# Normalised fp16 parts of x for the query, u and gate products of a hybrid attention and gMLP block, in a written order

## The chip, the cores and the metric

The kernel runs on one core of a Trainium2 chip. The metric is the time of one execution on the device in microseconds, and the figure for a kernel is the median of its runs. The core has five engines that run side by side, each with its own stream of instructions: PE (TensorE, the matrix products; its weight loads are listed apart as PEld), DVE (VectorE), ACT (ScalarE), POOL (GpSimd) and SP (SyncE, which issues most transfers). An instruction that needs another engine's result waits for it, and everything behind it on its engine waits too.

## The reference, cut to what matters

The block has 1024 tokens and a width of 1024. One projection of the RMS-normalised input feeds attention, a gated MLP over positions, and two merge gates.

```python
h = rmsnorm(x, norm_gain)                       # x * rsqrt(mean(x^2)) * gain
q, k, v, gate_a, u_in, v_in, gate_b, g_merge = split(h @ w_in)   # 512,128,128,512,512,512,512,2048
q = axial_rope(rmsnorm(q, q_gain)); k = axial_rope(rmsnorm(k, k_gain))   # 8 q heads, 2 kv heads, 64 each
attn = block_attention(q, k, v) * silu(gate_a)  # softmax over all 1024 keys
y_a = attn @ w_proj_attn
vv = layernorm(gelu(v_in)) in 8 chunks of 128 tokens, 8 groups of 64 channels
v_mix = w_spatial (128x128 per group) applied over the positions of a chunk, + b_spatial
gm = gelu(u_in) * v_mix * silu(gate_b)
y_b = gm @ w_proj_gmlp
g = sigmoid(g_merge + b_merge)                  # two gates, 1024 columns each
y = g[0] * y_a + g[1] * y_b
out = rmsnorm(x + y @ w_out, final_gain)
```

## The kernel before, in words

**Products in parts.** Every fp32 product is made of three matmuls: each operand is split into a rounded part (hi) and the remainder (lo), and `mm3` adds hi·hi, hi·lo and lo·hi in PSUM. In most of the kernel the parts are fp32r; in the softmax weights and in the merge gates they are fp16. A split is a cast on ACT (L112) and a subtraction (L118) on DVE or, for the weights of u, gate_a and gate_b, on POOL.

**x.** `load_x` brings the transposed x in eight tiles of 128 channels, multiplies by the gain and splits into `xh`, `xl` (fp32r, 16 tiles of 512 KB, resident until the gates). They are not yet normalised. The key-value, v, q, u, gate_a and gate_b products all read them, and the factor 1/rms of each token (`rstd`) is applied to each result: in the activation for v, in the head norms for q and k, and by a DVE multiply with the row `rB` after each u or gate product (L511, L494). The mean squares come from a second load of x, rows as tokens, squared on ACT (`add_square`, L171). `rB` is made at the end of the q products (L475).

**Stages.** The key-value products (`mm3` with 256 columns) run while x arrives. Then come four v groups and the position mixing `spatial` (sp), then four q groups with the head norm, the rotary table and transposes to `qT` (`q_post`). Attention is 64 units (one head, 128 queries): a score product (L550, L551) into one of three PSUM tiles of tag S, a row maximum on DVE (L553), an exponential on ACT (L557), a reciprocal, a hi part on ACT (L563) and a lo part on DVE (L564), and a transposing transfer T<-p on the SP queue. Two units make one `mix` with the values (L576). Between the units lie 24 **fills**: u, gate_a and gate_b, four column tiles each and two halves of 512 tokens, 24 matmuls a half (L488 to L490). Their weights come by `stream_w`: hi on ACT, lo on POOL. After attention come eight products with the gMLP projection (`proj_b`, yb), then for each of eight column tiles a pair of merge gates (`pair`, g) by a scheme with seven block products in place of eight (`seven`), the attention projection ya by the same scheme, and the output product with the final norm.

**Gates.** Before the gates x is loaded a third time and, chunk by chunk (`x_chunk`), normalised and made into the seven forms the scheme needs, each split to fp16 (`make_forms`). The weights of a pair are brought to unit size first: `pair_weights` loads two 512 KB tiles, squares them on ACT, sums over the partitions with four one-column matmuls (usg, L671), and POOL takes the power (L673 to L677, tile scg); `split16` then makes hi on ACT (L682) and lo on DVE (L683).

**Order.** The order of the work is that of the code as a scheduler then places it on each engine: `plan` spreads the fills over the units, and `MORDER` lists the gate and projection steps (in it, w0 stands right before g0).

## Time and profile before

| quantity | value |
|---|---|
| time, median of three runs | 736.19 us (736.14 to 736.78) |
| profiled execution, its own time | 736.99 us |
| span of the profiled execution | 735.2 us |
| PE busy | 714.0 us, 97% of the span |
| DVE, ACT, POOL busy | 565.9, 431.2, 110.4 us |
| granted PE clock, mean | 0.992 |

The profiled execution took 1.8 us more than its span and 0.8 us more than the median of the runs. Busy PE time contains the slack between pipelined matmuls, so that 97% does not say that PE runs at its best pace in every stage. The share of DVE is an average too: it differs from stage to stage.

The stages, as the first instruction of each on PE marks them, in microseconds from the start of the span: key-value and v products 5.4 to 82; q products, position mixing and k transposes 82 to 135.7; the first 32 score products 135.7 to 265.6; the others 265.6 to 386.7; gMLP projection 386.7 to 450.1; gates and attention projection 450.1 to 618.8; output 618.8 to 735.2.

### The profile page before, as it was taken

The page shows a single profiled execution, that of the slowest core. Times are in us where ns is not written, and L with a number is a line of the kernel's source. Part 1 is how long each engine was busy: PE and PEld are TensorE (multiplying, and loading weights), DVE is VectorE, ACT ScalarE, POOL GpSimd, SP SyncE. Part 2 cuts the span into 40 slices and gives each one's busy share as a digit, 9 for nine tenths or more (in the row PEclk, how much of TensorE's full clock was granted, in tenths as well). Part 3 has the DMA queues.
Part 4 walks back from the last instruction along what each step waited for, and adds up shares of the span by engine and source line. Part 5 has one row for each costly group of instructions (what it writes and reads, how often), then busy time and mean ns, then how long its engine had stood idle before and what let it go on. Part 6 is the DMA issues. An engine that isn't in the chain of part 4 may idle for free.

```text
span 735.2 us, 11836 instructions
## 1 busy us (share of the span) xinstructions
PE 714.0 (97%) x4633; PEld 531.4 (72%) x4633; DVE 565.9 (77%) x822; ACT 431.2 (59%) x770; POOL 110.4 (15%) x101
## 2 busy tenths in 40 slices
...
GB/s 307 317 129 1 115 16 43 1 122 94 150 157 182 176 180 167 183 170 175 154 245 287 132 30 14 45 129 15 46 98 58 0 1 184 157 146 1 114 30 86
DMA packets 152904, 85.59 MB, mean 116 GB/s; under 512 B 135440, under 2 KB 136080, under 8 KB 152848
## 3 DMA queue, kind: packets, MB, share of 16 engines
...
q10 hardware_dynamic: 288, 0.28, 0.1%
...
## 4 chain that ended last, share of the span: by engine, by line
PE 83%; DVE 5%; ACT 5%; DMA 5%; issue 1%; POOL 1%; SPq 0%; POOLq 0%; ACTq 0%; DVEq 0%
PE o L576 5%; PE out L175 4%; DMA T<-p 4%; PE out L176 4%; PE out L174 4%; PE s L550 3%; PE s L551 3%; PE g L174 3%; PE g L175 3%; PE g L176 3%; PE gb L488 2%; PE q L174 2%; PE q L175 2%; PE v L175 2%; PE v L174 2%; PE q L176 2%
## 5 line engine op out<-in xcount | busy, mean ns | idle before, releaser
L564 DVE SCALAR_TENSOR_TENSOR p<-P,ri,p 128x1024 f16<-128x1024 f32 x64 | 83.4, 1304 | 26.4 <-ACT p L563 26.3
L557 ACT ACTIVATE P<-s,nm 128x1024 f32<-128x1024 f32 x64 | 71.2, 1113 | 24.2 <-DVE nm L553 20.8
L563 ACT ACTIVATE p<-P,ri 128x1024 f16<-128x1024 f32 x64 | 73.1, 1145 | 15.7 <-DMA T<-p 8.8
L553 DVE TENSOR_REDUCE nm<-s 128x1 f32<-128x1024 f32 x64 | 77.6, 1214 | 3.0 <-PE s L551 2.9
L576 PEld LDWEIGHTS <-vS 128*64 128x64 f16 x1536 | 45.3, 111 | 19.0 <-issue 17.8
L576 PE MATMUL o<-T,vS 128*64 128x128 f16 x1536 | 52.0, 222 | 4.2 <-DMA T<-p 3.8
L118 POOL TENSOR_TENSOR wl<-wraw,wh 128x512 fp32r<-128x512 f32 x24 | 39.9, 1665 | 97.7 <-ACT wh L112 55.6
L550 PE MATMUL s<-kT,qT 128*128 128x512 f32 x128 | 52.9, 413 | 0.0
L551 PE MATMUL s<-kT,qT 128*128 128x512 f32 x128 | 50.9, 397 | 0.0
L911 ACT ACTIVATE sq<-xr 128x1024 f32<-128x1024 f32 x7 | 7.4, 1062 | 65.4 <-DVE xr L969 65.4
L969 DVE TENSOR_TENSOR xr<-out,xr 128x1024 f32<-128x1024 f32 x7 | 8.6, 1224 | 47.6 <-PE out L176 47.5
L674 POOL TENSOR_SCALAR scg<-scg 128x1 f32<-128x1 f32 x8 | 6.5, 807 | 206.7 <-ACT scg L673 206.6
L550 PEld LDWEIGHTS s<-kT,qT 128*128 128x128 f32 x128 | 24.3, 189 | 6.3 <-issue 0.2
L551 PEld LDWEIGHTS s<-kT,qT 128*128 128x128 f32 x128 | 24.3, 190 | 5.4 <-issue 0.2
L112 ACT CAST wh<-wraw 128x512 fp32r<-128x512 f32 x35 | 21.4, 616 | 10.4 <-PE ga L489 3.4
L682 ACT ACTIVATE wg<-graw,scg 128x512 f16<-128x512 f32 x16 | 11.4, 721 | 26.6 <-PE g L176 13.2
L488 PE MATMUL ga<-xh,wh 128*128 128x512 f32 x64 | 26.0, 406 | 0.8 <-DVE ga30w L494 0.5
L488 PE MATMUL u<-xh,wh 128*128 128x512 f32 x64 | 25.8, 402 | 0.0
L488 PE MATMUL gb<-xh,wh 128*128 128x512 f32 x64 | 25.5, 399 | 0.0
L175 PE MATMUL yb<-gml,wh 128*128 128x512 f32 x64 | 25.5, 398 | 0.0
L490 PE MATMUL u<-xh,wl 128*128 128x512 f32 x64 | 25.4, 397 | 0.0
L490 PE MATMUL gb<-xh,wl 128*128 128x512 f32 x64 | 25.4, 396 | 0.0
...
## 6 DMA issues: line engine op xcount, KB each, us to landing
...
graw<-in_wall_dram SPq DMA_DIRECT2D x16, 512.0 KB, 5.8
xraw<-in_xT_dram SPq DMA_DIRECT2D x13, 512.0 KB, 6.4
xn<-in_x_dram SPq DMA_DIRECT2D x8, 512.0 KB, 6.3
wor<-in_wall_dram SPq DMA_DIRECT2D x8, 512.0 KB, 5.1
xr<-in_x_dram SPq DMA_DIRECT2D x8, 512.0 KB, 3.8
out_dram<-xr SPq DMA_DIRECT2D x7, 512.0 KB, 2.6
...
```

What stands on the lines that cost most here:

```text
L174: pe.matmul(o, ah, bh, start=start, stop=False)
L175: pe.matmul(o, ah, bl, start=False, stop=False)
L176: pe.matmul(o, al, bh, start=False, stop=stop)
L488: pe.matmul(o, wh[:, C(dt % 4)], xh[dt][:, H(h)], start=(dt == 0), stop=False)
L490: pe.matmul(o, wl[:, C(dt % 4)], xh[dt][:, H(h)], start=False, stop=(dt == 7))
L550: pe.matmul(sp[:, H(hf)], qs, kT[:, 2 * v, H(hf)], start=True, stop=False)
L551: pe.matmul(sp[:, H(hf)], qs, kT[:, 2 * v + 1, H(hf)], start=False, stop=True)
L553: dve.tensor_reduce(out=nm, in_=sp, axis=AX.X, op=ALU.max, negate=True)
L557: act.activation(Pt, sp, AF.Exp, bias=nm, accum_out=rsum)
L563: act.activation(hi, Pt, AF.Copy, scale=ri)
L564: dve.scalar_tensor_tensor(out=lo, in0=Pt, scalar=ri, in1=hi, op0=ALU.mult, op1=ALU.subtract)
L576: pe.matmul(ot[64 * h:64 * h + 64, 0:128], vS[:, kt, v, 64 * vl:64 * vl + 64], T[:, h, 8 * p + kt, :], start=(n == 0), stop=(n == len(part ...
```

## The change

The fp32r parts `xh`, `xl` stay for the key-value and v products only. x is squared in its transposed tiles as it arrives (ACT, two of them on POOL), summed on DVE, and eight one-column matmuls (`sst`) give the mean squares, so that `rstd` and `rB` stand during the v products; the loads of x by rows are gone. The transposed x is loaded again in four pairs of 512 KB tiles, multiplied by `rB` (three tiles on DVE, five in halves on POOL) and split into resident fp16 parts `x16` (eight casts of 1024 on ACT, eight subtractions on DVE). q, u, gate_a and gate_b become fp16 products of `x16` with weights that are first scaled to unit size, as the gates already did. The scales need the weights once more: `scales` loads those of q and of the first four fill tiles in eight 512 KB transfers issued by the ACT queue, into the tiles of the squares, and those of the other eight in sixteen 256 KB transfers on the SP queue, and squares them on ACT. One group of four matmuls (usq) gives q's scale and the first four of the fills, three groups of two (usu, usa, usb) the others. `split16` makes their parts, hi on ACT and lo on DVE, in place of POOL's subtraction. The DVE multiply by `rB` after a fill is gone for the gates (`silu2` takes the scale in the Tanh) and is a multiply by a scalar for u; the scale of gate_b enters where gm is split, that of gate_a in `avs`. The gates take three of their seven forms from `x16`, so that `x_chunk` splits four and not seven. gm is split within the attention stage, and the weights of the first gate pair (`pair_weights(0)`) are prepared behind the third yb product. In place of `plan` and `MORDER` the order from the v products to the gates is written out as a sequence of calls.

```diff
-    BUFS = {"xh": 8, "xl": 8, "T16": 4, "vS": 1, "P": 2, "p16": 2, "og": 2, "rB": 1, "gg": 6}
+    BUFS = {"xa": 4, "T16": 4, "vS": 1, "P": 2, "p16": 2, "og": 2, "rB": 1, "gg": 6}
...
+    def tX(name, dt=F32R):
+        return t8("X", 8, name, dt)
+
+    def tX16(name):
+        return sb.tile([P, 2, 2, 1024], F16, tag="X", bufs=8, name=name)
 
...
+    def add_square(dt):
+        t = t4("xa", f"xsq{dt}")
+        if dt in SQPOOL:
+            pool.tensor_tensor(out=t, in0=xraw0[dt], in1=xraw0[dt], op=ALU.mult)
+        else:
+            act.activation(t, xraw0[dt], AF.Square)
+        if dt == 0:
+            ssq.append(t)
+        else:
+            (pool if dt in ADPOOL else dve).tensor_tensor(out=ssq[0], in0=ssq[0], in1=t, op=ALU.add)
+
+    SQPOOL, ADPOOL = (1, 4), ()
 
...
+    sst = ps_o("sst")
+    for tt in range(NT):
+        with tc.high_priority():
+            pe.matmul(sst[:, tt:tt + 1], ssq[0][:, C(tt)], ones[:, 0:1], start=(tt == 0), stop=(tt == NT - 1))
+    power_rstd(rstd, sst[:, 0:NT], NT, 1.0 / D)
...
+    rB = t4("rB", "rB")
+    with tc.high_priority():
+        rp = [ps_z("rb0"), ps_o("rb1")]
+        for tt in range(NT):
+            pe.matmul(rp[tt // 4][:, C(tt % 4)], rstdh[:, tt:tt + 1].broadcast_to([P, P]), identr.bitcast(F32),
+                      start=True, stop=True)
+        for h in range(2):
+            dve.tensor_copy(rB[:, H(h)], rp[h])
+
...
+    def split16(hi, lo, raw, sc, how):
+        act.activation(hi, raw, AF.Copy, scale=sc)
+        dve.scalar_tensor_tensor(out=lo, in0=raw, scalar=sc, in1=hi, op0=ALU.mult, op1=ALU.subtract)
...
+    def load_pair(k):
+        xpair[k] = t8("qT", 4, f"xp{k}", F32)
+        for i in range(2):
+            nc.sync.dma_start(out=xpair[k][:, i, :], in_=xT[C(2 * k + i), :])
+
+    def norm_part(dt):
+        raw = xpair[dt // 2][:, dt % 2, :]
+        if dt in NPD:
+            dve.tensor_tensor(out=raw, in0=raw, in1=rB, op=ALU.mult)
+            return
+        for h in range(2):
+            pool.tensor_tensor(out=raw[:, H(h)], in0=raw[:, H(h)], in1=rB[:, H(h)], op=ALU.mult)
+
+    NPD = (0, 1, 3)
+
+    def norm_split(dt):
+        raw = xpair[dt // 2][:, dt % 2, :]
+        if dt < 4:
+            t = sb.tile([P, 2, 1024], F16, tag="xa", bufs=BUFS["xa"], name=f"x16{dt}")
+        else:
+            if dt % 2 == 0:
+                x16["t"] = tX16(f"x16{dt}")
+            t = x16["t"][:, dt % 2]
+        split16(t[:, 0, :], t[:, 1, :], raw, gs[:, dt:dt + 1], "dve")
+        x16[dt] = t
+
+    order = ["u2", "a0", "u0", "b1", "u1", "u3", "a1", "b0", "b2", "b3", "a2", "a3"]
+    base = {"a": 0, "u": 4, "b": 8}
+    ws, wsc = {}, {}
...
+    def scales(names, tags=None):
+        n = len(names)
+        k = names[0]
+        ss = const([P, n, 8], f"ss{k}")
+        s0, s1 = const([P, n], f"s0{k}"), const([P, n], f"s1{k}")
+        if tags is not None:
+            pool.memset(ss, 0.0)
+        for i, o in enumerate(names):
+            blocks = range(W_Q, W_Q + 4) if o == "q" else [W_TR + base[o[0]] + int(o[1])]
+            for j, blk in enumerate(blocks):
+                if tags is not None:
+                    raw = t4(tags.pop(0), f"sq{o}{j}")
+                    nc.scalar.dma_start(out=raw, in_=wall[blk])
+                    act.activation(raw, raw, AF.Square, accum_out=ss[:, i, j:j + 1])
+                    continue
+                for h in range(2):
+                    raw = load_w(blk, h)
+                    act.activation(raw, raw, AF.Square, accum_out=ss[:, i, 2 * j + h:2 * j + h + 1])
+        if tags is None:
...
+    def scales_end(names, ss, s0, s1):
+        k, n = names[0], len(names)
+        nscale.append(k)
+        pt = ps_oz(len(nscale), f"us{k}")
+        used = 4 if "q" in names else 2
+        with tc.high_priority():
+            for j in range(used):
+                pe.matmul(pt[:, 0:n], mscale.broadcast_to([P, P]), ss[:, :, j], start=(j == 0), stop=(j == used - 1))
+        act.copy(s1, pt[:, 0:n])
+        pool.tensor_scalar(out=s1, in0=s1, scalar1=1.0, scalar2=1e-30, op0=ALU.mult, op1=ALU.add)
+        pool.tensor_tensor(out=s0, in0=s1, in1=mhalf[:, 0:n], op=ALU.pow)
...
+    def nat_part(o, dt, tt, w):
+        mm3(o, x16[dt][:, 0, C(tt)], x16[dt][:, 1, C(tt)], w[0], w[1], dt == 0, dt == 7)
 
...
+    def prep_q(dt):
+        if dt % 4 == 0:
+            wqt[0] = sb.tile([P, 4, 2, 512], F16, tag="ptr", bufs=2, name=f"wq{dt}")
+        raw = load_w(W_Q + dt // 2, dt % 2)
+        wq.append((wqt[0][:, dt % 4, 0, :], wqt[0][:, dt % 4, 1, :]))
+        split16(*wq[dt], raw, wsc["q"][0], "dve")
...
+        sp = ps_s(f"q{g}")
+        for dt in range(8):
+            for k in range(2):
+                nat_part(sp[:, H(k)], dt, 2 * g + k, wq[dt])
+        qsts[g] = t4(QST[g], f"qst{g}")
         act.copy(qsts[g], sp)
...
+    def prep(k, et):
+        name = f"{k}{et}"
+        if not wt:
+            w = sb.tile([P, 2, 2, 2, 512], F16, tag="X", bufs=8, name=f"w{name}")
+            wt.extend(w[:, k] for k in range(2))
+        t = wt.pop(0)
+        sc = wsc[name]
+        for i in range(2):
+            raw = load_w(W_TR + base[k] + et, i)
+            split16(t[:, i, 0, :], t[:, i, 1, :], raw, sc[0], "dve")
+        ws[k, et] = t, sc[1]
+
...
-    def z_mm(o, ws, h, dts=range(8)):
-        for dt in dts:
-            wh, wl = ws[dt // 4]
...
-
-    def silu2(zp, h, name):
-        w = t2(f"{name}w")
-        dve.tensor_tensor(out=w, in0=zp, in1=rB[:, H(h)], op=ALU.mult)
+    def z_mm(o, ws, h):
+        for dt in range(8):
+            wh, wl = (ws[:, dt // 4, k, C(dt % 4)] for k in range(2))
+            pe.matmul(o, wh, x16[dt][:, 0, H(h)], start=(dt == 0), stop=False)
+            pe.matmul(o, wh, x16[dt][:, 1, H(h)], start=False, stop=False)
+            pe.matmul(o, wl, x16[dt][:, 0, H(h)], start=False, stop=(dt == 7))
+
+    def silu2(zp, sc, name):
         t = t2(f"{name}t")
-        act.activation(t, w, AF.Tanh)
-        dve.scalar_tensor_tensor(out=t, in0=t, scalar=1.0, in1=w, op0=ALU.add, op1=ALU.mult)
+        act.activation(t, zp, AF.Tanh, scale=sc)
+        dve.scalar_tensor_tensor(out=t, in0=t, scalar=1.0, in1=zp, op0=ALU.add, op1=ALU.mult)
         return t
 
     def fill_u(et, h, ws):
...
-        dve.tensor_tensor(out=w, in0=zp, in1=rB[:, H(h)], op=ALU.mult)
+        dve.tensor_scalar(out=w, in0=zp, scalar1=sc, scalar2=None, op0=ALU.mult)
...
+    def gm_split(et):
+        t = tX(f"gm{et}")
+        gmh.append(t[:, 0, :])
+        gml.append(t[:, 1, :])
+        sc = bsc[et]
+        act.activation(gmh[et], vm[:, et, :], AF.Copy, scale=sc)
+        dve.scalar_tensor_tensor(out=gml[et], in0=vm[:, et, :], scalar=sc, in1=gmh[et].bitcast(F32),
+                                 op0=ALU.mult, op1=ALU.subtract)
...
+        for key, dt, h in (("11", j, 0), ("22", j + 4, 1), ("21", j + 4, 0)):
+            XB.setdefault(key, []).append((x16[dt][:, 0, H(h)], x16[dt][:, 1, H(h)]))
 
     def halves_of(t):
...
+    v_group(0)
...
+    load_wsp(0)
+    early = scales(["q"] + order[:4], ["xa"] * 8)
+    load_pair(1)
+    load_wsp(1)
+    load_pair(2)
+    load_pair(0)
+    norm_part(3)
+    v_group(1)
+    ktmp = t4("vS", "ktmp")
+    head_norm(kn, ktmp, 0, 8, "kf")
+    v_group(2)
+    with tc.high_priority():
+        scales_end(*early)
...
+    scores(*hs[0])
+    prep_next()
+    v_affine(3)
+    prep_next()
+    scales(order[10:12])
+    scores(*hs[1])
+    scores(*hs[2])
+    scales(order[8:10])
+    scores(*hs[3])
+    v_affine(2)
+    run_fill(*halves[0])
+    prep_next()
+    scores(*hs[4])
+    q_norm(2)
...
+    proj_b(2)
+    load_chunk(2)
+    load_chunk(3)
+    pws[0] = pair_weights(0)
+    proj_b(3)
...
```

**Three places where instructions move.** In the rows that follow, each line is one instruction or a run of equal ones (x2, x4) in the order in which its engine takes them: the line of the kernel, the operation, the result and its operands.

The first is ACT during the key-value and v products. Here xn is x by rows, nh a part of v's weights, wsh one of the spatial weights, kn the keys, and sqq, squ, sqa, sqb are weights loaded for their squares (of q, u, gate_a and gate_b). Before:

```order
L204 COPY kn<-kv_89 128x256
L112 CAST nh_414<-wraw_421 128x512
L204 COPY kn<-kv_90 128x256
L112 CAST nh_430<-wraw_428 128x512
L204 COPY kn<-kv_89 128x256
L112 CAST nh_430<-wraw_436 128x512
L204 COPY kn<-kv_90 128x256
L171 ACTIVATE xn_418,ssx<-xn_418 128x1024
L171 ACTIVATE xn_425,ssx<-xn_425 128x1024
L171 ACTIVATE xn_433,ssx<-xn_433 128x1024
L112 CAST wsh<-wspr_464 128x512
L112 CAST wsh<-wspr_468 128x512
```

Now:

```order
L350 ACTIVATE sqq_560,ssq<-sqq_560 128x1024
L349 DMA squ_569<-in_wall_dram 128x1024
L349 DMA sqb_572<-in_wall_dram 128x1024
L350 ACTIVATE squ_563,ssq<-squ_563 128x1024
L118 CAST wsh<-wspr_578 128x512
L237 COPY kn<-kv_88 128x256
L237 COPY kn<-kv_89 128x256
L237 COPY kn<-kv_88 128x256
L350 ACTIVATE sqa_566,ssq<-sqa_566 128x1024
L350 ACTIVATE squ_569,ssq<-squ_569 128x1024
L237 COPY kn<-kv_89 128x256
L350 ACTIVATE sqb_572,ssq<-sqb_572 128x1024
```

The squares of x by rows are gone from here, and in their place stand squares of weights whose transfers ACT issues itself. What reads their sums on PE stands within the v products (now):

```order
L189 MATMUL v_589<-nl_172,xhl_176 128x512
L190 MATMUL v_589<-nh_254,xhl_176 128x512
L188 MATMUL v_589<-nh_254,xhl_221 128x512
L366 MATMUL usq<-ssq,mscale 128x5 x4
L189 MATMUL v_589<-nl_172,xhl_221 128x512
L190 MATMUL v_589<-nh_254,xhl_221 128x512
```

The four usq matmuls stand inside the second of the four v groups on PE's stream, and the rest of the group stands behind them.

The second is DVE at the first score products. nm is a row maximum, ri a reciprocal, p the lo part of the softmax weights, qf and qst and qtmp the head norm and rotary products of q, wa the lo part of a gate_a weight. Before:

```order
L553 TENSOR_REDUCE nm_1365<-s_1360 128x1
L312 TENSOR_TENSOR qf_1528<-qf_1528,rsq 128x16
L133 TENSOR_SCALAR qf_1528<-qf_1528 128x16
L553 TENSOR_REDUCE nm_1383<-s_1378 128x1
L560 RECIPROCAL ri_1370<-ri_1370 128x1
L314 TENSOR_TENSOR qf_1528<-qf_1528,rstd 128x16
L315 TENSOR_TENSOR qst_1239<-qst_1239,qf_1528 128x1024
L553 TENSOR_REDUCE nm_1400<-s_1395 128x1
L326 TENSOR_TENSOR qtmp_1526<-qst_1239,tabq 128x16x16
L564 SCALAR_TENSOR_TENSOR p_1373<-P_1367,ri_1370,p_1373 128x1024
L560 RECIPROCAL ri_1388<-ri_1388 128x1
```

Now:

```order
L640 TENSOR_REDUCE nm_1599<-s_1594 128x1
L424 TENSOR_TENSOR qst_1279<-qst_1279,qf_1715 128x1024
L651 SCALAR_TENSOR_TENSOR p_1531<-P_1525,ri_1528,p_1531 128x1024
L613 TENSOR_TENSOR avs<-s1a_1352,vsc 128x1
L647 RECIPROCAL ri_1587<-ri_1587 128x1
L303 SCALAR_TENSOR_TENSOR wa_1686<-wraw_1687,s0a_1351,wa_1686 128x512
L435 TENSOR_TENSOR qtmp_1713<-qst_1279,tabq 128x16x16 x4
L303 SCALAR_TENSOR_TENSOR wa_1686<-wraw_1691,s0a_1351,wa_1686 128x512
L303 SCALAR_TENSOR_TENSOR wa_1686<-wraw_2594,s0a_1351,wa_1686 128x512
L303 SCALAR_TENSOR_TENSOR wa_1686<-wraw_2598,s0a_1351,wa_1686 128x512
L640 TENSOR_REDUCE nm_1640<-s_1635 128x1
L438 TENSOR_TENSOR qst_1279<-qst_1279,tabq 128x1024
```

Four subtractions for gate_a weights, which POOL made before, now stand between two row maxima on DVE, and so does the whole rotary product of a q group.

The third is PE ahead of the first gate. usg is the group of one-column matmuls of a gate pair's scale, g a product of the gates. Before:

```order
L174 MATMUL yb_5442<-gmh,wh_5445 128x512
L175 MATMUL yb_5442<-gml_5094,wh_5445 128x512
L176 MATMUL yb_5442<-gmh,wl_5446 128x512
L671 MATMUL usg_5486<-gss_5477,mscale 128x1 x2
L671 MATMUL usg_5640<-gss_5631,mscale 128x1 x4
L174 LDWEIGHTS wg_5505
L174 MATMUL g_5508<-xf_5146,wg_5505 128x512
```

Now:

```order
L188 MATMUL yb_5374<-gm_5198,wh_5377 128x512
L292 MATMUL usg_5358<-gss_5349,mscale 128x1 x4
L189 MATMUL yb_5374<-gm_5198,wh_5377 128x512
L190 MATMUL yb_5374<-gm_5198,wl_5378 128x512
L188 MATMUL yb_5374<-gm_5025,wh_5377 128x512
L189 MATMUL yb_5374<-gm_5025,wh_5377 128x512
...
L190 MATMUL yb_5564<-gm_5198,wl_5568 128x512
L188 LDWEIGHTS wg_5598
L188 MATMUL g_5601<-x_721,wg_5598 128x512
```

The usg group of the first gate pair moved from right before the first g product to 110 matmuls ahead of it.

759 lines of the change are left out of this document (475 added, 284 removed).

## The prediction

> **What bounds the kernel now.** I read the page's head and the chain of waits first, for the engine that ends last; then a table of stages, for where that holds; then PE's list of waits, for what it stands still for.
>
> ```profile
> span 735.2 us, 11836 instructions
> PE 714.0 (97%) x4633; PEld 531.4 (72%) x4633; DVE 565.9 (77%) x822; ACT 431.2 (59%) x770; POOL 110.4 (15%) x101
> PE 83%; DVE 5%; ACT 5%; DMA 5%; issue 1%; POOL 1%; SPq 0%; POOLq 0%; ACTq 0%; DVEq 0%
> ```
>
> ```profile
> core 0: us, PE busy (x) PEld busy (x) DVE busy (x) ACT busy (x) POOL busy (x), PEclk, DMA share, GB/s
> 5.40:82.00 76.60, 75.84 (x444) 66.56 (x443) 49.46 (x104) 42.73 (x71) 9.70 (x9) 1.00 0.53 188
> 82.00:135.70 53.70, 53.70 (x279) 45.12 (x278) 41.54 (x64) 28.01 (x48) 11.64 (x7) 1.00 0.11 35
> 135.70:265.60 129.90, 124.45 (x1079) 98.48 (x1078) 115.38 (x148) 101.29 (x196) 35.87 (x20) 0.99 0.71 136
> 265.60:386.70 121.10, 121.10 (x1221) 97.66 (x1220) 97.98 (x127) 96.76 (x175) 30.08 (x19) 1.00 0.97 183
> 386.70:450.10 63.40, 56.37 (x329) 44.83 (x327) 60.99 (x91) 40.58 (x76) 5.11 (x6) 0.97 0.48 127
> 450.10:618.80 168.70, 168.69 (x795) 92.77 (x796) 144.43 (x220) 90.70 (x164) 12.90 (x27) 0.99 0.15 51
> 618.80:735.20 116.40, 109.51 (x479) 81.71 (x477) 54.63 (x66) 28.25 (x40) 4.37 (x8) 0.99 0.28 104
> 137.80:179.70 41.90, 37.70 (x259) 29.44 (x258) 39.96 (x54) 29.61 (x60) 13.80 (x7) 1.00 0.47 95
> 440.00:460.00 20.00, 13.80 (x63) 7.47 (x62) 18.25 (x24) 11.97 (x20) 6.64 (x8) 0.83 0.07 21
> ```
>
> ```profile
> PE g L174 <- ACT wg L682: 6.2, 1, 6.2
> PE o L576 <- DMA T<-p: 3.8, 3, 3.1
> ```
>
> The chain is 83% PE, but the stages differ. In the q products, the second half of attention and the gates PE is busy in all of the stretch: there only fewer or shorter matmuls help. In the first half of attention DVE has 115.4 us of work in 129.9, and in its first 41.9 us it is busy 39.96, or 0.954, while PE has gaps: DVE sets the pace. Ahead of the gates PE stands 6.2 us for the first gate weight, and the granted clock is 0.83 around it.
>
> **From the start to the first score product (135.7 us before).** Pitches come from the timeline: the first and last of a run of matmuls, divided by the steps.
>
> ```profile
> 111.10 0.40 PE L174 MATMUL q<-nh,xh 128*128 128x512 f32 x1
> ...
> 115.89 0.39 PE L174 MATMUL q<-nh,xh 128*128 128x512 f32 x1
> ```
>
> ```profile
> 470.35 0.38 PE L174 MATMUL g<-xf,wg 128*128 128x512 f16 x1
> ...
> 475.53 0.38 PE L174 MATMUL g1T<-xfT,wg1T 128*128 128x512 f16 x1
> ```
>
> ```profile
> 109.78 0.28 PE L175 MATMUL sp<-wsl,vh 128*128 128x256 f32 x1
> ...
> 110.98 0.28 PE L176 MATMUL sp<-wsh,vl 128*128 128x256 f32 x1
> ```
>
> The fp32r products take 4.79 / 21 = 0.2281 us each, the fp16 ones of the gates 5.18 / 24 = 0.2158, those with 256 columns 1.20 / 10 = 0.12. So 192 q products in fp16 save 192 x 0.0123 = 2.4 us. Against that stand 22 new small matmuls (eight sst, eight rB, four usq, two usu):
>
> ```profile
> 500.89 0.56 PE usg L671 x6
> L475 PE MATMUL rb<-dg,ones x4: 592/592/592, 134.4 to 135.6; 128*128 128x512 f32 x4
> ```
>
> The first row holds two records a matmul, so 0.19 each, or 4.1 us; the old rb, some 1.8 us, leaves: +2.3. Eight query transposes move behind the first score, −0.9 by the 0.12 of 256 columns.
>
> The new wait here is usq. It needs the squares of eight weight tiles, which take turns in four tiles with the squares of x, so they begin when x is through:
>
> ```profile
> 25.87 1.28 DVE L159 SCALAR_TENSOR_TENSOR xl<-xraw,cs,xh 128x1024 fp32r<-128x1024 f32 x1 [0.98 <-ACT xh L158]
> L171 ACT ACTIVATE xn<-xn 128x1024 f32<-128x1024 f32 x8 | 8.5, 1064 | 4.4 <-DMA xn<-in_x_dram 4.2
> ```
>
> ```profile
> xn<-in_x_dram SPq DMA_DIRECT2D x8, 512.0 KB, 6.3
> wor<-in_wall_dram SPq DMA_DIRECT2D x8, 512.0 KB, 5.1
> ```
>
> No row shows such loads on ACT's queue, so I bound them by the 512 KB loads of SP's. With a landing of L and two in flight (ACT's stream alternates loads and squares), the eight take 4 L from 26 us, and some five squares of 1.06 us are not covered by a transfer: 31.3 + 4 L, which is 51.7 for the 5.1 of the weight loads and 56.5 for the 6.3 of x. PE reaches usq after 192 products of 256 columns, 67 of v and 16 small ones: 5.4 + 23.0 + 15.3 + 3.0 = 46.7. Where the first loads find a free tile before x is through, the wait is nothing, and at 6.3 it is 10 us. I take 4, nearest to the row of weight loads (5.0), less a little since PE itself will be late. Two and a half v groups stand behind usq on PE, so the wait is paid in full. The normalising (eight casts, eight subtractions of 1024, 13 multiplies) I cost at nothing here: DVE and ACT were busy 91 and 71 of the 130 us, and position mixing covers it; without cover DVE alone would add some 10. The sum: 135.7 − 2.4 + 2.3 − 0.9 + 4 = 138.7.
>
> **First score to the 33rd (129.9).** DVE's own rows decide; the first three are groups of this stretch alone, the others of the whole run.
>
> ```profile
> L494 DVE TENSOR_TENSOR gb11w<-gb,rB 128x512 f32<-128x512 f32 x1 | 0.7, 682 | 0.0
> L312 DVE TENSOR_TENSOR qf<-qf,rsq 128x16 f32<-128x16 f32 x2 | 1.4, 717 | 0.0
> L564 DVE SCALAR_TENSOR_TENSOR p<-P,ri,p 128x1024 f16<-128x1024 f32 x30 | 39.9, 1331 | 9.6 <-ACT p L563 9.6
> L564 DVE SCALAR_TENSOR_TENSOR p<-P,ri,p 128x1024 f16<-128x1024 f32 x64 | 83.4, 1304 | 26.4 <-ACT p L563 26.3
> L341 DVE TENSOR_TENSOR qs<-qst,qs 128x512 fp32r<-128x512 f32 x8 | 6.9, 881 | 0.9 <-ACT qs L340 0.9
> L683 DVE SCALAR_TENSOR_TENSOR wg<-graw,scg,wg 128x512 f16<-128x512 f32 x16 | 11.9, 747 | 3.8 <-ACT wg L682 3.2
> L118 POOL TENSOR_TENSOR wl<-wraw,wh 128x512 fp32r<-128x512 f32 x24 | 39.9, 1665 | 97.7 <-ACT wh L112 55.6
> L311 DVE TENSOR_REDUCE qf<-qtmp 128x16 f32<-128x1024 f32 x4 | 4.8, 1212 | 3.0 <-ACT qtmp L307 3.0
> ```
>
> In the changed order twelve fill-weight lows (0.747 by the same form in L683) stand in this stretch, which were POOL's: +9.0. One more head reduction (+1.2), one more q split (+0.9) and three lows of yb weights (+2.0, by the 0.68 of L494, a subtraction or product of the same size) too. Out go four gate multiplies (4 x 0.68 = −2.7) and, in two head norms, two small products like L312 each, for one that is shorter (about −2.5). 115.4 becomes 123.3. Some of it gets shorter without POOL's subtraction beside it: L564 takes 1331 ns here and (83.4 − 39.9) / 34 = 1279 elsewhere: 30 x 0.052 = 1.6 us. That is the whole of it in this row, and the bounds are nothing and the length of POOL's ten subtractions here, 17 us; I stay with the row, since it is DVE's most frequent work. At 0.954 busy 121.7 us need 127.6; less some 2.6 of DVE work (a maximum and a lo part) that the last score products of the stretch, three in a row in the new order, leave behind the 33rd: 125. The fills there, 267 products in fp16, save 3.3 us of PE behind DVE and count nothing; were PE the bound, they would count.
>
> A rule bears on POOL's half. The Trainium skill ("SBUF — State Buffer", section "Who interferes with whom") says that a DVE instruction with two SBUF inputs contends with a GpSimd instruction that reads SBUF for a shared port, which one of them holds for the whole instruction. The 52 ns of L564 are little for that, so the trace bears the rule out weakly; by the rule alone the relief could reach the 17 us of the upper bound, and the stage would fall to PE's own pace, the first rival below.
>
> **33rd score to the first yb (121.1).** PE is the bound, with DVE at 98 us. 285 fp16 fill products save 3.5; one more mix stands here than before, and three fill products fewer (−0.7):
>
> ```profile
> L576 PE MATMUL o<-T,vS 128*64 128x128 f16 x1536 | 52.0, 222 | 4.2 <-DMA T<-p 3.8
> ```
>
> A mix is 48 of these, 52.0 / 32 = 1.6 us. 121.1 − 3.5 + 1.6 − 0.7 = 118.5.
>
> **First yb to the first gate (63.4).**
>
> ```profile
> 444.83 3.84 POOL L674 TENSOR_SCALAR scg<-scg 128x1 f32<-128x1 f32 x2 [67.10 <-ACT scg L673]
> ```
>
> usg, its copy, POOL's steps (the row is the first two of them) and the cast follow one another, and PE stands for them. With usg 110 products (110 x 0.228 = 25 us) earlier the chain of 6 us is covered, and DVE loses twelve form splits and the gm splits, so it is ready too. Out go the 6.2 and the other idle time (63.40 − 56.37 − 6.2 = 0.8), and about 1.5 us of the low clock after the stall: 55. The gates' and the output's products are unchanged: 168.7 and 116.4.
>
> **The sum.** 138.7 + 125 + 118.5 + 55 + 168.7 + 116.4 = 722.3 us of span, against 735.2. The profiled execution took 736.99, its span + 1.8, and the median lies 0.8 below it: 723.3, or 723 us.
>
> **Rivals.** (1) *PE alone sets the pace of early attention, and usq costs nothing.* The second half, 118.5, less 18 fill products (3.9) and six mixes (9.8), plus 56 transposes at 0.06 to 0.12 and small ones (some 5), is about 110; with 3 us for the first T<-p transfer, 113. Then 134.7 + 113 + 118.5 + 55 + 168.7 + 116.4 = 706, time 707. For it: POOL's 40 us gone from beside DVE. Against: DVE's count goes up, and its rows hardly show POOL. 0.18. (2) *The wait ahead of the gates stays*, because DVE, at 60.99 of 63.40 there, still has its forms to make: +7, 730. Against: its work there shrinks by a third. 0.07. (3) *The fp16 products run at the fp32r pitch*: +2.4 + 3.5, 729; the gates' pitch speaks against it. 0.03. (4) *DVE's added work counts in full*: early attention 129.9 + 7.9 = 137.8, nothing gained by POOL: 736, no change. 0.05. (5) *Slower: the scale loads starve the front.* ACT's loads queue behind one another while v's weights and the reloaded x use the same transfers at 188 GB/s. Taken one at a time at 6.3 they end at 26 + 50 = 76 us, PE stands 31 us inside the v groups, and the time is 750; it turns slower from a wait of 17 us. Against it: with two in flight that would need L = 8, above the longest row, and the order has two loads side by side. 0.07.
>
> **How the numbers follow.** The forecast has 0.60: 723, and by its own unknowns (usq 0 to 10, early attention 116 to 132) some 712 to 733, both ends not being met at once. The range reaches down to rival 1 and up past rival 2: 707 to 734. A difference of 0.2%, or 1.5 us, is about what a measurement of this kernel can tell from none. Faster gathers the forecast and rivals 1 to 3, 0.88; no change is rival 4 and what is near it, 0.05; slower 0.07.
>
> **What would show it.** On the page after: PE idle at usq by 0 to 10 us in the second v group; q and fill pitches of 0.216; the first score near 139; DVE over 0.93 busy in the first 40 us of attention and the 33rd score near 264; the first yb near 382; no wait on wg, and the first gate near 437. A first score after 150, or a 33rd more than 132 us behind it, would prove me wrong.

## The result: slower by 1.4%

The changed kernel takes 747.23 us (median; 744.80 to 748.41) against 736.49 (736.14 to 737.95) for the one before: a ratio of 1.0138, with a 95% interval of 1.0108 to 1.0167. The forecast was 723. The profiled execution took 748.41 us, with a span of 746.6; it is the longest of the four. In what follows "before" and "changed" are the two kernels, and a ratio of any other kernel is to the time of before, measured beside it on the same chip.

The page's head and chain of waits of the changed kernel:

```profile
span 746.6 us, 12013 instructions
PE 713.0 (95%) x4685; PEld 471.2 (63%) x4685; DVE 591.8 (79%) x824; ACT 452.6 (61%) x808; POOL 132.3 (18%) x118
PE 47%; DVE 20%; DMA 11%; ACT 10%; issue 7%; POOL 4%; SPq 1%; POOLq 0%; DVEq 0%; ACTq 0%
```

PE's share of the chain fell from 83% to 47%. PE is still the largest part, but DVE, transfers and ACT together now hold 41%.

The table of stages, first of the changed kernel, then for its front the same stretches of before:

```profile
core 0: us, PE busy (x) PEld busy (x) DVE busy (x) ACT busy (x) POOL busy (x), PEclk, DMA share, GB/s
4.90:57.60 52.70, 47.32 (x304) 42.83 (x302) 40.26 (x55) 34.80 (x54) 10.32 (x6) 0.94 0.84 303
57.60:100.00 42.40, 34.85 (x160) 27.78 (x160) 39.37 (x53) 19.49 (x27) 30.95 (x25) 0.92 0.14 45
100.00:146.00 46.00, 43.45 (x237) 25.74 (x236) 39.09 (x69) 34.69 (x62) 11.97 (x10) 0.96 0.42 137
156.80:283.00 126.20, 120.99 (x1039) 73.69 (x1039) 115.27 (x157) 106.03 (x207) 27.59 (x22) 0.97 0.75 147
283.00:408.60 125.60, 121.02 (x1279) 74.92 (x1278) 101.84 (x125) 94.25 (x171) 11.12 (x8) 1.00 0.89 158
408.60:462.70 54.10, 53.74 (x323) 41.84 (x322) 47.99 (x73) 32.25 (x59) 16.17 (x4) 1.00 0.51 142
```

```profile
5.40:57.60 52.20, 51.44 (x312) 45.35 (x312) 33.15 (x65) 30.53 (x51) 4.19 (x4) 1.00 0.69 250
57.60:100.00 42.40, 42.40 (x229) 36.68 (x228) 31.13 (x68) 23.20 (x37) 8.37 (x8) 1.00 0.17 54
```

From 57.6 to 100 us PE was busy all the time before; now it is busy 34.85 of 42.40 us with 160 matmul records for 229, and its clock is 0.92. DVE (39.37 for 31.13) and POOL (30.95 for 8.37) have the work that was added. By markers on PE:

| us from the span's start | before | forecast | changed |
|---|---|---|---|
| first score | 135.7 | 138.7 | 156.8 |
| first yb | 386.7 | 382.2 | 408.6 |
| first gate | 450.1 | 437.2 | 462.7 |
| first output | 618.8 | 605.9 | 630.9 |
| end | 735.2 | 722.3 | 746.6 |

So the front lost 21.1 us, the stretch from first score to first gate gained 8.5 (314.4 to 305.9, all of it and more behind the first yb: 63.4 to 54.1), and what follows gained 1.2. PE's list of waits of the changed kernel (line waited for: total us, times, longest us):

```profile
PE q L188 <- ACT vst L481: 7.5, 1, 7.5
PE s L637 <- ACT P L644: 2.7, 2, 1.4
PE v L188 <- DVE vn L238: 2.5, 1, 2.5
PE q L188 <- ACT qst L538: 2.5, 1, 2.5
PE kv L189 <- DVE wl L124: 2.1, 1, 2.1
PE o L663 <- DMA T<-p: 0.9, 2, 0.5
```

The 6.2 us for wg are gone, and T<-p went from 3.8 to 0.9; usq, where the forecast put its wait, is not in the list at all. The greatest wait is new: the first q product waits for a gelu of v. The timeline around it (start, duration, engine, instruction, then in brackets the idle time before it and its releaser), from ACT, DVE, SP's queue and PE:

```profile
85.76 1.32 ACT L302 ACTIVATE wq<-wraw,s0q 128x512 f16<-128x512 f32 x2
89.73 1.15 ACT L302 ACTIVATE x<-xp,gs 128x1024 f16<-128x1024 f32 x1 [0.67 <-POOL xp L318]
95.63 0.72 ACT L302 ACTIVATE wq<-wraw,s0q 128x512 f16<-128x512 f32 x1 [4.75 <-DMA wraw<-in_wall_dram]
96.26 1.25 ACT L481 ACTIVATE vst<-v,rstd 128x512 f32<-128x512 f32 x2
...
91.99 0.71 DVE L303 SCALAR_TENSOR_TENSOR wq<-wraw,s0q,wq 128x512 f16<-128x512 f32 x1
...
92.73 0.33 SPq L128 DMA_DIRECT2D wraw<-in_wall_dram  x1
...
97.55 0.59 PE L188 MATMUL q<-wq,x 128*128 128x512 f16 x1 [7.54 <-ACT vst L481]
97.93 0.63 PE L189 MATMUL q<-wq,x 128*128 128x512 f16 x1
...
102.62 0.63 PE L188 MATMUL q<-wq,x 128*128 128x512 f16 x1
103.05 0.54 PE L189 MATMUL q<-wq,x 128*128 128x512 f16 x1
```

The gelu frees the PSUM tile that q wants. It stands in ACT's stream behind the cast of a third q weight half; that half was loaded only at 92.73, right after DVE's subtraction at 91.99 had let go of one of the four raw weight tiles; and DVE was late. After the stall the products run at a step of 0.427 us (12 steps from 97.93 to 103.05), which is twice the 0.216 of the q products behind them; the granted clock of this stretch is 0.50. Before, the clock had fallen like this in two places only: behind a wait of 3.1 us for T<-p (180 to 184 us) and ahead of the gates. The Trainium skill ("TensorE: Matmul & The Clock Gate", section "What's actually happening") says that an idle window of about 3.4 us halves the clock and about 3.4 us of sustained work restores it. The half clock and the long stall agree with that; the lengths here do not fit closely. The low clock lasted through 5.5 us of products, and stalls shorter than the window were followed by a low clock as well: one of 2.1 us (kv, at 16.55 us) from 18 to 21 us, and one of 2.5 us by double steps from 52.42 to 55.41 us:

```profile
50.85 0.47 PE L188 MATMUL v<-nh,xhl 128*128 128x512 f32 x1 [2.51 <-DVE vn L238]
...
52.42 0.63 PE L188 MATMUL v<-nh,xhl 128*128 128x512 f32 x1
```

### The profile page after: what moved, and what is told of

The parts are those of the page before. It is cut to its first block, busy times and chain, and to the rows that moved or that the text cites. A ratio compares the mean times of both kernels' runs of the same rounds, so it can differ in the third digit from the quotient of the medians.

```text
span 746.6 us, 12013 instructions
## 1 busy us (share of the span) xinstructions
PE 713.0 (95%) x4685; PEld 471.2 (63%) x4685; DVE 591.8 (79%) x824; ACT 452.6 (61%) x808; POOL 132.3 (18%) x118
## 4 chain that ended last, share of the span: by engine, by line
PE 47%; DVE 20%; DMA 11%; ACT 10%; issue 7%; POOL 4%; SPq 1%; POOLq 0%; DVEq 0%; ACTq 0%
DMA T<-p 5%; PE out L189 4%; PE out L190 4%; PE out L188 4%; DVE p L651 4%; DVE nm L640 3%; PE g L188 3%; PE g L190 3%; PE g L189 3%; ACT p L650 2%; DMA sqq<-in_wall_dram 2%; DMA xraw<-in_xT_dram 2%; ACT P L644 2%; PE o L663 1%; DMA wraw<-in_wall_dram 1%
## 5 line engine op out<-in xcount | busy, mean ns | idle before, releaser
L640 DVE TENSOR_REDUCE nm<-s 128x1 f32<-128x1024 f32 x64 | 77.4, 1212 | 1.3 <-PE s L638 1.3
L637 PE MATMUL s<-kT,qT 128*128 128x512 f32 x128 | 56.7, 443 | 3.5 <-ACT P L644 2.7
L638 PE MATMUL s<-kT,qT 128*128 128x512 f32 x128 | 50.8, 397 | 0.0
L189 PE MATMUL out<-wo,yhl 128*128 128x512 f32 x96 | 37.4, 392 | 0.0
L188 PE MATMUL out<-wo,yhl 128*128 128x512 f32 x96 | 37.3, 392 | 0.0
L190 PE MATMUL out<-wo,yhl 128*128 128x512 f32 x96 | 37.3, 390 | 0.0
L188 PE MATMUL g<-x,wg 128*128 128x512 f16 x96 | 36.4, 379 | 0.0
L189 PE MATMUL g<-x,wg 128*128 128x512 f16 x96 | 36.4, 379 | 0.0
L190 PE MATMUL g<-x,wg 128*128 128x512 f16 x96 | 36.4, 379 | 0.0
L188 PE MATMUL q<-wq,x 128*128 128x512 f16 x64 | 25.5, 398 | 10.1 <-ACT vst L481 7.5
L637 PEld LDWEIGHTS s<-kT,qT 128*128 128x128 f32 x128 | 24.3, 190 | 12.1 <-ACT P L644 3.8
L188 PE MATMUL v<-nh,xhl 128*128 128x512 f32 x64 | 25.8, 403 | 2.5 <-DVE vn L238 2.5
L596 POOL TENSOR_TENSOR vm<-vm,ut 128x512 f32<-128x512 f32 x8 | 13.4, 1675 | 82.7 <-DVE ut L382 42.3
```

The lines of the kernel that those rows point to most:

```text
L188: pe.matmul(o, ah, bh, start=start, stop=False)
L189: pe.matmul(o, ah, bl, start=False, stop=False)
L190: pe.matmul(o, al, bh, start=False, stop=stop)
L596: pool.tensor_tensor(out=vm[:, et, H(h)], in0=vm[:, et, H(h)], in1=t, op=ALU.mult)
L637: pe.matmul(sp[:, H(hf)], qs, kT[v][:, 0, H(hf)], start=True, stop=False)
L638: pe.matmul(sp[:, H(hf)], qs, kT[v][:, 1, H(hf)], start=False, stop=True)
```

## The experiments

The theory at the start: the front, not attention, costs the time, through the work on DVE and ACT that the forecast had counted at nothing. The rivals: the scales' loads, POOL beside DVE, and the reading of PSUM banks in the fills.

Two things limit these comparisons. First, every edit lets the scheduler place the instructions anew. Counted by the tiles that the matmuls write, from 115 (g2) to 439 (f4) of the changed kernel's 4685 are gone or stand elsewhere in the kernels made from it; e2 differs from f4 by 355 and from f1 by 235. So a difference is that of an edit together with the order that it brings. Nearly free of this are only e1 against before (26 matmuls elsewhere) and e3, f2 and f3 among themselves (21 between e3 and the other two, none between f2 and f3). What the written order costs by itself was not tested. Second, the marks of one trace move. `e5` has the changed kernel's streams up to 194 us, and yet its first q product stands at 95.8 us and its first score at 155.1, for 97.6 and 156.8.

### The gain behind the first yb, alone

Kernel before, with only the first gate pair's weights prepared early:

```diff
+        if dt == 2:
+            pws[0] = pair_weights(0)
...
-    for step in MORDER.split():
+    for step in MORDER.split()[1:]:
```

> The kernel before with one thing of the change: the weights of the first gate pair are prepared behind the third yb product. Theory 'the 9.3 us that the change wins between the first yb and the first gate come from this place alone': the 6.2 us wait, the other idle time and the low clock go, 728 us against 736.5. Rival 'VectorE, 61 of 63.4 us busy there, holds the first gate anyway' (the change wins there by the form splits it leaves out): 734 to 736.

It took 731.85 us, a ratio of 0.9927 (0.9908 to 0.9946): 5.2 us faster than before, and the fastest of all kernels here. From first yb to first gate it took 56.3 us for 63.4, in this row:

```profile
386.00:442.30 56.30, 55.30 (x321) 43.79 (x319) 55.83 (x84) 37.00 (x69) 2.16 (x4) 1.00 0.53 143
PE usg L671 <- ACT gsq L806: 1.6, 3, 0.8
```

That part of the forecast (55) holds, alone and in the whole change (54.1). But the gates and the output take 288.6 us here for 285.1, so 3.5 of it came back; the second row shows a new wait for the squares of the next pair. A second kernel takes this wait away too, by loading and squaring pair 1 after `dt == 5` and leaving its sums where they were:

```diff
+        if dt == 5:
+            pwl[1] = pair_weights(1)
```

> The kernel before with the first gate pair's weights prepared behind the third yb product (731.9 alone) and the loads, squares and scale of the second pair behind the sixth. That first run won 7 us up to the first gate and lost 3.5 behind it, where PE stands for the second pair's squares (usg, gsq) inside the first pair's products. If that wait is the loss, 728 to 729; if the loss is VectorE's work in the first gates, 731 to 732.

It took 734.13 us, 0.9961 (0.9948 to 0.9975): no better. The wait for gsq is gone and others stand there:

```profile
PE g L176 <- DVE wg L683: 1.2, 1, 1.2
PE g0T L174 <- DVE gb L698: 1.2, 1, 1.2
443.20:481.00 37.80, 34.04 (x158) 15.33 (x158) 34.43 (x52) 22.81 (x37) 2.83 (x6) 1.00 0.08 28
```

Behind the first gate DVE is busy 34.43 of 37.80 us, so that gates which begin earlier wait for DVE: for the lo part of a gate weight (L683) and for a sum of block products (L698). Why exactly 3.5 us come back is not settled.

### The scales

In `e2` a constant (1448) stands in place of every scale of the q and fill weights: no second loads of these weights, no squares of them, no usq and its like.

```diff
-    early = scales(["q"] + order[:4], ["xa"] * 8)
+    early = None
...
+        pool.memset(s0, KSC)
...
-    scales(order[4:6])
```

> The changed kernel without finding the scales of the q and fill weights: their 8 loads on the ACT queue, 16 on SP's, the squares and the usq, usu, usa, usb matmuls are left out and one constant is used in their place. Theory 'transfers': the loads, which keep the transfers at 300 GB/s up to 57 us, are what makes the front late; the front loses the 10 us up to usq and the weights of q are ready earlier, 730 to 735 us. Theory 'VectorE in the front is full': only the small matmuls and some squares go, 742 to 745.

It took 736.06 us, 0.999 (0.9975 to 1.0005): 11 us less than the changed kernel, the largest effect of one part. The first score comes at 146.5 for 156.8. Its first two stages:

```profile
4.90:57.60 52.70, 49.26 (x319) 44.84 (x319) 43.13 (x63) 26.45 (x38) 20.05 (x14) 1.00 0.62 225
57.60:100.00 42.40, 37.51 (x181) 28.50 (x180) 41.98 (x55) 24.83 (x34) 24.59 (x22) 0.96 0.18 62
```

ACT has 26.45 us to do up to 57.6 us, for 34.80. The clock is 1.00 up to there, but so it is in e3 below, which keeps the squares. `f4` is e2 with the eight early loads put back on ACT's queue, into the same tiles, and nothing that reads them:

```diff
+            raw = t4("xa", f"sq{o}{blk}")
+            nc.scalar.dma_start(out=raw, in_=wall[blk])
```

> The kernel without scales (736.1), but with the eight 512 KB loads on the ACT queue done all the same, into the same tiles, and read by nobody. Theory 'transfers': the loads alone bring back most of the 11 us, 743 to 746, and the key-value and v products end near 86 us. Theory 'squares and the chain from usq to the weights of q': the loads cost little, 736 to 738.

It took 733.04 us, 0.995 (0.9934 to 0.9966), 3 us *less* than without the loads, with the first score at 146.6. So the transfers show no cost. ACT's waits for them, in the changed kernel and then in f4:

```profile
ACT sqq L350 <- DMA sqq<-in_wall_dram: 8.7, 4, 3.0
ACT squ L350 <- DMA squ<-in_wall_dram: 2.4, 2, 1.8
```

```profile
ACT nh L118 <- DMA sqq<-in_wall_dram: 5.7, 1, 5.7
ACT kn L237 <- DMA sqq<-in_wall_dram: 1.8, 1, 1.8
```

Between 26 and 54 us the changed kernel's ACT stands 11.7 us (with 0.6 for sqb) until a square's load has landed. In f4 it still stands 7.5 us, since an issue in ACT's stream waits for an earlier load there, and f4 is not slower for it. What f4 leaves out is the other 4.2 us and the squares themselves. The fifth rival had the right direction and nearly the right time (750), but the wrong cause: PE did not stand at usq, and the loads alone cost nothing. Why f4 is 3 us faster than e2 is not explained; its order is another one, with one mix and 24 fill products more behind the first yb than in e2.

Next, the wait on the result. In `i1` all scales are found as before, but q and the first four fill weights use a constant, so that nothing waits for the first chain; in `i2` the first group is found and used, and the eight later scales are constants, without their loads and squares:

```diff
+        const_scale(["q"] + order[:4])
...
+    for names in (order[4:6], order[6:8], order[8:10], order[10:12]):
+        const_scale(names)
-    scales(order[4:6])
```

> The changed kernel with a constant as the scale of q and of the first four fill weights, while their loads, squares, usq and POOL's powers are all still done and read by nobody. Theory 'the weights of q wait for the chain of the scale' (736.1 without any scales): most of the 10 us of the front come back, the first score near 148 and 738 to 741. Theory 'it is the work of the scales (ACT's squares, POOL's steps, the late sixteen squares)': 745 to 748.

> The changed kernel with a constant for the other eight fill weights: their sixteen 256 KB loads, sixteen squares on ACT and usu, usa, usb are left out between 120 and 175 us, the first group stays. Theory 'ACT between the q products and the first scores' (16 squares of 0.6 us and their loads in the ring of raw tiles): 741 to 743, the first score some 3 us earlier. Theory 'only the first group costs': 746 to 748.

`i1` took 748.49 us, 1.016 (1.0133 to 1.0187): that the weights wait for the first scales costs nothing that this run shows (the usq matmuls keep a place in PE's stream in it). `i2` took 742.32, 1.0066 (1.0046 to 1.0086): the later eight, with the order that goes with them, cost 5 us. What is left of the 11, some 6 us, is the first group's work; that is by exclusion and was not measured alone. Most of it is likely to be the eight squares in ACT's stream ahead of 57.6 us, behind which casts for k and v stand: eight of 1.06 us are 8.5, near to the 8.35 by which the ACT column differs. The changed kernel's row for four of them, and for such a load (KB, then us from issue to landing):

```profile
L350 ACT ACTIVATE sqq<-sqq 128x1024 f32<-128x1024 f32 x4 | 4.2, 1061 | 8.7 <-DMA sqq<-in_wall_dram 8.7
...
sqq<-in_wall_dram ACTq DMA_DIRECT2D x4, 512.0 KB, 5.8
```

### Normalising: POOL or DVE

`e3` gives all eight tiles to DVE (`NPD = tuple(range(8))`, for `(0, 1, 3)`).

> The changed kernel with all eight multiplications of x by rB on VectorE, none on POOL. Theory 'POOL beside VectorE': L303 takes up to 2.4 us and L315 1.7 beside POOL's halves against 1.25 and 1.20 without, and the powers wait behind the halves; without them 3 to 5 us are won, 742 to 745. Theory 'VectorE in the front is full': five products of 1.2 us more, 750 to 753.

It took 743.20 us, 1.0088 (1.0071 to 1.0105): 4 us less, though DVE has five products more to make. The first score comes at 146.3, 10.5 us earlier, but only 4 are left in the medians, and 6.7 in the spans of the two profiled executions (739.9 for 746.6). The groups of lines of DVE and POOL from 42 to 140 us (busy us, mean ns), changed kernel, then e3:

```profile
L303 DVE SCALAR_TENSOR_TENSOR x<-xp,gs,x 128x1024 f16<-128x1024 f32 x8 | 12.1, 1530 | 0.1
L315 DVE TENSOR_TENSOR xp<-xp,rB 128x1024 f32<-128x1024 f32 x3 | 4.6, 1572 | 0.0
L318 POOL TENSOR_TENSOR xp<-xp,rB 128x512 f32<-128x512 f32 x10 | 14.7, 1501 | 7.7 <-DVE rB L283 7.7
```

```profile
L303 DVE SCALAR_TENSOR_TENSOR x<-xp,gs,x 128x1024 f16<-128x1024 f32 x8 | 10.2, 1272 | 0.0
L315 DVE TENSOR_TENSOR xp<-xp,rB 128x1024 f32<-128x1024 f32 x8 | 9.6, 1221 | 0.0
```

DVE's own products are on average 260 to 350 ns faster once POOL's are gone. In the changed kernel single ones take far more than the mean (least, median, longest, in ns):

```profile
L315 DVE TENSOR_TENSOR xp<-xp,rB x3: 1199/1212/2306, 59.4 to 66.6; 128x1024 f32<-128x1024 f32 x3
```

Two things may lie in that: POOL's reads slow DVE, or POOL's queue is late for others (it also takes the powers). Two kernels on top of e3 give POOL dead work of about the same length, written into a tile that is not yet in use: products that read, or memsets that only write.

```diff
+            if dt not in (0, 1, 3):
+                for h in range(2):
+                    pool.tensor_tensor(out=vm[:, 3, H(1)], in0=raw[:, H(h)], in1=rB[:, H(h)], op=ALU.mult)
```

> All eight multiplications by rB on VectorE, and POOL does ten products of 128x512 beside them, after each of the five tiles, whose results nobody reads. Theory 'POOL's reads hold VectorE': L303 and L315 take 1.5 us again in place of 1.25, and the first score moves from 146 by 5 us or more, 746 to 750. Theory 'x16 waited for POOL's result in the changed kernel': with no one waiting for the products the first score stays near 147 and the time at 743 to 744.

```diff
+            if dt not in (0, 1, 3):
+                pool.tensor_tensor(out=vm[:, 3, 512:513], in0=raw[:, 0:1], in1=rB[:, 0:1], op=ALU.mult)
+                for h in range(6):
+                    pool.memset(vm[:, 3, H(1)], 1.0 + h)
```

> As the run with ten products on POOL, but with thirty fills of 128x512 with a constant (some 0.5 us each by the 128x128 of the start, 205 ns) in place of the products: POOL is busy as long and its powers wait as long, but it reads nothing. Theory 'reads hold VectorE': L303 and L315 stay at 1.25, the time within 1 us of the 743.2 without them. Theory 'the powers of the layer norm wait behind POOL's work': as slow as with the products.

Reads: 752.28 us, 1.0209 (1.0193 to 1.0224). Writes: 747.62, 1.0147 (1.0117 to 1.0177). The groups, of the kernel with reads, then of that with writes:

```profile
L318 POOL TENSOR_TENSOR vm<-xp,rB 128x512 f32<-128x512 f32 x10 | 19.0, 1896 | 5.3 <-DVE xp L315 4.8
L303 DVE SCALAR_TENSOR_TENSOR x<-xp,gs,x 128x1024 f16<-128x1024 f32 x8 | 12.6, 1570 | 0.0
```

```profile
L319 POOL MEMSET vm<- 128x512 f32 x30 | 16.3, 543 | 1.6
L303 DVE SCALAR_TENSOR_TENSOR x<-xp,gs,x 128x1024 f16<-128x1024 f32 x8 | 10.1, 1268 | 0.0
```

Beside POOL's memsets the DVE instruction takes the 1268 ns that it takes with no POOL work (1272); beside POOL's products it takes 1570. So reading counts and writing does not, and it is worth up to 4.7 us of the whole time; the matmuls stand in the same order in both kernels. A part of the 4.7 may be queue: POOL's products took 19.0 us and its memsets 16.3. The occupied queue is worth about as much (747.62 − 743.20 = 4.4). That reads count and writes do not is what the Trainium skill's rule ("SBUF — State Buffer", section "Who interferes with whom") says of a shared port; the prediction had weighed it for the POOL work that left the fills, where the row showed 52 ns, and not for the ten halves that came, where it is 260.

The two effects do not add up. Without scales and with all eight tiles on DVE (`f1`, e2 and e3 together):

> The changed kernel with both edits: the scales not found but a constant in their place (736.1 alone), and all multiplications by rB on VectorE (743.2 alone), against 747.2. Theory 'two causes that add up' (scales 11, POOL's halves 4): 732, the first score near 136 where each alone gave 146. Theory 'one resource, VectorE and its chain, which each edit only relieves in its own way': less than the sum, 735 to 738, the first score near 143.

It took 741.98 us, 1.0068 (1.0047 to 1.0089), which is 5.9 us *more* than e2. Its first score comes earlier than that of any other kernel made from the changed one, at 143.5, but it takes 314.7 us from there to the first gate, for 304.8 in e2. PE's waits show `qtp L461 <- DVE qs L453` with 3.6 us as the longest; the rest is spread. Moving the products to DVE came with a gain beside the scales and with a loss without them. Whether that is the work or the order, in which 235 matmuls stand elsewhere than in e2, is not settled.

### Is it the amount of work on DVE?

`g1` leaves out the lower parts of `x16` (the products read the upper part twice), which takes about 12 us off DVE in the front; `g2` leaves out the lower parts of the fill weights in the same way; `g3` is g1 with e3; `h4` leaves out the lower parts of the q weights. The number of matmuls is the same in all four.

```diff
-        split16(t[:, 0, :], t[:, 1, :], raw, gs[:, dt:dt + 1], "dve")
+        act.activation(t[:, 0, :], raw, AF.Copy, scale=gs[:, dt:dt + 1])
...
```

> The changed kernel without the eight subtractions of 1024 that make the lower parts of x16 (1530 ns each in its trace); the products read the upper part in both places, so no matmul is left out, and the values of q, the fills and three gate forms are not the reference's. Theory 'VectorE is full from 57 us on' (39.4 of 42.4 us busy up to 100): its 12 us go from the chain to the q products, the first score comes near 146 and the time near 736 to 739. Theory 'the chain through usq and POOL's powers': the first score moves by 3 us or less, 744 to 747.

> Both: no lower parts of x16, and the multiplications by rB all on VectorE (743.2 alone). Theory 'VectorE's own work plus what POOL's reads add to it': 12 - 6 us less work for it than in the changed kernel and no instruction lengthened, so 4 to 8 us below the run without the lower parts' 736 to 739 if that holds: 731 to 734, first score near 139. Theory 'the scales are the next limit right behind VectorE': no better than the run without lower parts alone.

```diff
-            split16(t[:, i, 0, :], t[:, i, 1, :], raw, sc[0], "dve")
+            act.activation(t[:, i, 0, :], raw, AF.Copy, scale=sc[0])
...
```

> The changed kernel without the 48 subtractions of 512 for the weights of u, gate_a and gate_b (two a tile half pair, 0.75 us each), which POOL made before; the fills read the upper part in both places, so no matmul is left out. Theory 'VectorE in front and early attention': some 28 of them lie ahead of the 33rd score, 21 us of VectorE; with half of that on the path 735 to 739. Theory 'PE sets the pace of attention': only the few in the front count, 743 to 746.

| | time, us | ratio (95%) | first score | first score to first gate |
|---|---|---|---|---|
| changed | 747.23 | 1.0138 (1.0108 to 1.0167) | 156.8 | 305.9 |
| g1, no lower parts of x | 747.09 | 1.0131 (1.0112 to 1.0151) | 153.2 | 308.4 |
| g3, the same with e3 | 744.08 | 1.0101 (1.0081 to 1.0121) | 148.4 | 306.5 |
| g2, none of the fill weights | 745.64 | 1.0120 (1.0099 to 1.0141) | 153.6 | 306.3 |

Neither kind moves the time by more than 1.6 us (g3 has to be read against e3: 744.08 and 743.20). The stage from the first to the 33rd score in g2, which answers to 156.80 to 283.00 in the changed kernel, and g1's greatest wait:

```profile
153.57:278.75 125.18, 119.89 (x1038) 73.53 (x1037) 107.59 (x145) 102.93 (x200) 28.40 (x22) 0.97 0.76 145
```

```profile
PE q L188 <- ACT vst L481: 6.0, 1, 6.0
```

DVE has 7.7 us less to do in early attention (107.59 for 115.27), and the stage gets only 1.1 us shorter (125.2 for 126.3), at the same clock; three fill products that left it, 0.6 us, are part of that. So removing DVE work hardly shortens the stage any longer. The wait at the start of q stays as well (6.0 us in g1).

The opposite test lets DVE copy each fill's PSUM bank first, so that Tanh and the product read the copy and the bank is free sooner; that is 0.7 us of DVE more for each of 16 halves:

```diff
+        w = t2(f"{name}w")
+        dve.tensor_copy(w, zp)
...
-        act.activation(t, zp, AF.Tanh, scale=sc)
+        act.activation(t, w, AF.Tanh, scale=sc)
...
```

> The changed kernel with a VectorE copy of each gate fill out of PSUM, as the multiplication by rB was one before, so that the one bank of the fills comes free before the Tanh. Theory 'the bank is held too long': the waits of PE for ga11t, ga20t and ga01t (2.6 us) go and something of the clock, 743 to 745. Theory 'VectorE sets the pace of attention': 16 copies of 0.68 us more, 750 to 755.

It took 753.06 us, 1.0215 (1.0194 to 1.0237), 6 us more; the spans of the profiled executions differ by 2.6 (749.2 for 746.6). PE's waits for the fills' banks (2.6 us in the changed kernel: ga11t, ga20t, ga01t) are gone, and this one is there:

```profile
PE o L665 <- DMA T<-p: 6.8, 6, 2.0
```

The likely reading is that more DVE work makes the softmax parts late, and with them the transposing transfers; the copy also lengthens each fill's own chain, and the two were not told apart. So attention is not free of DVE: taking work away gives little, and adding 11 us cost 6 by the medians.

### The chain ahead of the first q product

Three kernels break single links of the chain that the timeline showed, and a fourth several: `h1` makes the cast of the third q weight half on DVE and not on ACT, `h2` puts `bias_term(1)` right behind `bias_term(0)`, `h3` is both of these with e3, and `h4` (above) makes the q weights cheap for DVE.

```diff
+        if dt == 2:
+            dve.tensor_scalar(out=wq[dt][0], in0=raw, scalar1=wsc["q"][0], scalar2=None, op0=ALU.mult)
...
```

> The changed kernel with the cast of the third q weight half on VectorE in place of ACT. In its trace the last two gelus of v (L481) stand on ACT behind that cast, the cast waits until 95.6 us for a load, and PE's first q product waits 7.5 us for the gelu, whose result frees its PSUM tile. Theory 'order on ACT': q starts near 92, PE loses 4 to 6 us less, 741 to 744. Theory 'the q weights themselves come late': q starts earlier and stands later, the first score within 2 us of 156.8, 746 to 748.

> The changed kernel with the second column sum of the spatial weights (bias_term) right behind the first, in front of the q weights. In the changed kernel it runs at 110 us and holds one of the four raw weight tiles until then, so that q's weights go through three. Theory 'the ring of raw tiles paces the q weights': the last q weight, 109 us before, comes 4 us or more earlier and so does the first score, 741 to 744. Theory 'not the ring': 746 to 748.

> Three edits of the front at once: multiplications by rB on VectorE (743.2 alone), the third q weight cast on VectorE, the second column sum early. Theory 'a chain of waits through one in-order engine after another, each edit shortens it': first score at or below 143, 738 to 741. Theory 'each takes away the same slack': 743.

> The changed kernel without the eight lower parts of q's weights (0.73 us each on VectorE); the q products read the upper part in both places, no matmul is left out, q is not the reference's. The raw tiles are then freed by ACT's cast and no longer wait for VectorE. Theory 'VectorE's place in the ring of raw tiles makes the loads late': q starts before 92, the first score near 148, 738 to 742. Theory 'VectorE has nothing to do with it' (as leaving out the lower parts of x moved the time by nothing): 745 to 747.

| | time, us | ratio (95%) | first q | first score | first score to first gate |
|---|---|---|---|---|---|
| changed | 747.23 | 1.0138 (1.0108 to 1.0167) | 97.6 | 156.8 | 305.9 |
| h1 | 747.82 | 1.0138 (1.0117 to 1.0160) | 92.3 | 153.6 | 308.2 |
| h2 | 748.52 | 1.0149 (1.0131 to 1.0167) | 97.5 | 155.2 | 309.6 |
| h3 | 745.97 | 1.0119 (1.0072 to 1.0166) | 88.9 | 148.5 | 307.4 |
| h4 | 747.07 | 1.0136 (1.0109 to 1.0164) | 92.7 | 153.2 | 308.2 |

```profile
92.34 0.59 PE L188 MATMUL q<-wq,x 128*128 128x512 f16 x1 [4.64 <-ACT vst L481]
```

This is h1's first q product: it starts 5.2 us earlier, the first score 3.2 us earlier, and the stretch behind that is 2.3 us longer. h4 and g1 show the same: 3.6 us less in front, 2.3 to 2.5 more behind. Against e5's marks, which are those of the changed kernel's own streams in a second trace, the first q product is still 3.5 us earlier in h1 and 3.1 in h4, but the first score only 1.5 and 1.9. The chain is real, since two of the three single links taken away (h1, h4) move the first q product by more than the traces move by themselves, but no price of its own shows: the intervals, some 2 us wide to each side, would hide a gain of 1 or 2 us. What takes back the rest is not settled. The kernels in which the stretch behind the first score is shorter are those without the later scales (e2 304.8, f4 301.5, i2 302.5). Their granted clock in the first 44 us of attention is 1.00, where it is 0.92 in the changed kernel and in g1 and 0.96 in h1 and h4; 0.08 of 44 us is 3.5 us. In the changed kernel it is 0.50 from 165 to 171 us, right behind two waits of 0.7 and 1.3 us and two groups of small products for these scales (usa, usb). f1, without scales, at 314.7 and with 0.92, is against a simple rule, but there the clock falls behind other waits of PE (1.4 and 3.6 us).

## Why the prediction was wrong

The sum missed by 746.6 − 722.3 = 24.3 us: +18.1 in the front, +8.3 from first score to first yb, −0.9 from there to the first gate, −1.2 behind it.

**The step that failed: "The normalising ... I cost at nothing here: ... position mixing covers it", and with it the squares of the weights, which have no term but PE's wait for their sum.** The cover was counted as a mean over 130 us, where DVE and ACT had had 39 and 59 us free. The work comes in one stretch, 57.6 to 100 us, after rB stands (51.9 us) and ahead of the first q product (97.6); DVE is 39.37 of 42.40 us busy there. Nor did the mixing stand where it was to cover: 24 of its products stand ahead of the first q product, for 48 before. From the end of v (85.9) to the first score the forecast left 59.4 us (its own counts put the end of v at 79.3) and it took 70.9: +11.5, of which 7.5 are the wait at q and 2.7 the 13 q products at the double step. In the same way the squares of the weights were priced only by when PE would wait for their sum, and not by the ACT time that they take from the casts for k and v. By e2 the scales' work moves the first score by 10.3 us (156.8 to 146.5). The forecast without its 4 us for usq is 134.7, so that 11.8 us of the front are left without any scale; the normalising is the work that stands there, but no run leaves it out whole. g1 took 12 us of its subtractions off DVE and moved the first score by 3.6, or by 1.9 against e5's mark. In the whole time the experiments put 11 us on the scales' work and 4 on POOL's share of the normalising, and since f1 shows that these do not add up, they are no two terms of one sum. That these two terms were missing is shown; how the loss divides between them, and what of it is the order, stays open.

**The wait at usq (+4, 0 to 10).** There was none. PE passed usq at 56.9 us, where the forecast had it at 46.7 without the wait and 50.7 with it: PE itself was late, by waits on k and v operands (2.1 + 2.5 us) and a clock of 0.94. The result of usq holds nothing up either (i1). So PE was 10.2 us later there than without a wait, just past the end of the range of 0 to 10, and for another reason: the mechanism was wrong, and that the size comes near is chance. The four loads of q's weights landed as bounded (5.8 us, between 5.1 and 6.3), two of the others did not (7.7 for u, 8.6 for b); the loads alone cost nothing (f4).

**"DVE sets the pace" in early attention (125).** It did before, with 0.954 in the first 41.9 us. In the changed kernel it is 115.27 of 126.20, or 0.913, and g2 shows that the stage does not follow DVE's work. The length came out near the forecast (126.3 from the first to the 33rd score for 125), but not as DVE's work over a share of 0.954: that is luck. The length rules out rival 1 (113) and rival 4 (137.8). An estimate from the steps in the traces (0.23 us a score product, 0.227 a fill product before and 0.216 now, 0.085 a query transpose, 0.034 a mix product) gives the stage some 113 us of PE work, so that it loses some 13; before it was 115 and 12. The border at 265.6 in the prediction was misread, too: the 33rd score of before stands at 262.7, so its early half took 127.0 and its late half 124.0.

**Late attention bound by PE (118.5).** It took 125.6. The fills did get shorter: PE's need there fell from some 123 to some 120 us by the same estimate, but its loss rose by about 4 us: PE's list of waits for this stage, empty before, now has 3.0 us for the one PSUM bank of the fills (ga11t, ga20t, uw) and 1.4 for a score tile (`s <- ACT P`). The forecast took the stage's 100% of busy PE as a bound that would come down with the products, and left no room for the waits that begin once PE is faster.

**Right.** The fp16 pitch (0.216 for q and for the fills, for the forecast's 0.2158), so that the third rival is out. The stretch ahead of the gates (54.1 for 55; the change of place alone gives 56.3, e1), so that the second is out. The gates and the output, forecast as unchanged: 283.9 for 285.1. The saving that the products were to bring is there in PE's need, by the estimate above; PE waits it away. And the sign by which the prediction would fall, a first score after 150, is the one that came.
